# A decoder layer with PEER retrieval: another layout and place for the expert gates, more row gathers before the last stage, and scores computed a tile ahead

## The chip, the cores and the metric

The kernel runs on one core of a Trainium2 chip. The metric is the device time of one execution in microseconds (us); the kernel before takes 1810.99 us, the median of three runs (1809.59 to 1811.35).

## The reference

The layer handles 512 tokens of width 1024. Its first half (differential attention, an mLSTM branch, gates, an output projection) is not touched. The second half is PEER, a retrieval of single-neuron experts from a table of 128 x 128:

```
q = (ht @ w_q).reshape(T, 8, 2, 64)
s = einsum('thpd,pnd->thpn', q, sub_keys)
sv, si = top_k(s, 16)                      # per half key
cand = sv[:, :, 0, :, None] + sv[:, :, 1, None, :]
cv, ci = top_k(cand, 16)
eidx = i1 * 128 + i2                       # 16 experts of each of 8 heads
g = softmax(cv)
act = gelu(einsum('cd,chkd->chk', hc, u_tab[eidx]))
out = einsum('chk,chkd->cd', g * act, v_tab[eidx])
```

A residual, a scale by the condition's gate row (`gt2`) and a last LayerNorm follow.

## The kernel before, in words

The tokens are four tiles of 128. For tiles 1 to 3 (384 tokens) the kernel works densely: for each of the 128 expert blocks it multiplies all tokens by the block's 128 u rows, applies gelu, multiplies by a gate matrix that is zero where an expert was not chosen, and multiplies the result by the block's 128 v rows. Tile 0 is handled sparsely: for each of its 128 slots (8 heads x 16 experts) POOL gathers one u row per token with an indirect DMA of 512 KB (`fetch`, L861), and DVE takes the dot product with the hidden row (`dots`, L869); later 128 gathers of v rows are added up into `accg` (`sparse`, L1227). A generator is advanced by `some` (L882), with a credit, wherever the program has room for it.

Products are exact to about float32 by splitting each operand into two float16 parts and three matmuls (`mm3_one`). So each weight block that comes in as float32 (`raw`, `vraw`) is split by ACT (high part) and DVE (low part), `split` L167.

The stages that matter here:

* **Routing** (`route`, L940), one tile after the other. DVE picks the top 16 of every half key from the scores `sb` (L916 to L921), then the top 16 of 80 candidate sums, then builds one-hot matrices for 8 groups of 16 tokens (L1026 to L1037). PE turns each group into gates (`tr<-onehot`), ACT copies them into half of a staging tile (`gstage`, L1050) and writes them to DRAM as `gd` (L1054). The staging tile has two halves, so a group's first copy waits for the write of the group two before. PE's spare time is filled by u blocks 0 to 71, whose gelu results go to DRAM as `actd`. The scores of a tile's first bank are computed at the end of the tile before (tiles 2 and 3), those of the others one bank ahead (L941 to L947). In tiles 1 to 3 a dot of tile 0 is done after each bank and each group: 39 of the 128 in all. They use two gather buffers.
* **The stage change.** When routing is through, `h2d` (the hidden row's scale, saved earlier) is loaded, the row `gt2` is made by PE transposes (`gate_row`, L1188), six gate loads are issued, and then the first u block round.
* **The expert stage.** 32 rounds of 4 blocks; the order is rounds 18 to 31 and then 0 to 17. The first 14 compute their u products (`u_round`, L1270); the last 18 are "held", that is, their activations are loaded from `actd` (`act_load`). `v_round` (L1308) multiplies by v. `gate` (L1279) multiplies a round's activations `at` by the gates `gblk` on DVE and splits them. A gate block serves two rounds and comes in four loads of 384 KB (`gate_load`, L1254); `ahead` (L1262) issues loads two rounds early. Gathers per block: `SP_V` = 1 in a v block and `SP_U` - `SP_V` = 1.8 in a u block. In the last round (`last_part`) the rest of `sparse` is drained, with tile 0's final LayerNorm (`finish`).

All plain loads are issued by SP in one queue, in the order that the scheduler sets; ACT issues the writes to DRAM and POOL the gathers. Each engine works through its instructions in a fixed order, so an instruction that waits holds back all behind it.

Of the kernel before, what the change touches and what calls it, by code (L numbers as in the profile page):

```python
# [10 lines left out]
F32 = mybir.dt.float32  # L11
# [48 lines left out]
DOT_R = 1  # L60
SP_U = 2.8
SP_0 = 0
# [44 lines left out]
def body(tc, x, c, w_ada, b_ada, wz, wif, b_if, conv_w, conv_b, lam, subg, mlg,  # L107
# [6 lines left out]
    with pool(name="cst", bufs=1) as cst, pool(name="wts", bufs=1) as wts, \  # L114
# [222 lines left out]

        h2d = dr.tile([128, 1024], F32, name="h2d")
        with pool(name="fr", bufs=1) as fr:
# [499 lines left out]
        actd = dr.tile([N1 // 2, 128, 2 * TD], F32, name="actd")  # L839
        gd = dr.tile([TD // 16, 16, 128, 128], F32, name="gd")  # L840
        RU = 1.0 / (S_ACT * S_U)
# [19 lines left out]
        def fetch(table, e, k):  # L861
            b = ring["buf"]
            g_ = b[:, ring["n"] % b.shape[1]]
            ring["n"] += 1
            P.before(G.indirect_dma_start(out=g_, out_offset=None, in_=table,  # L865
                                          in_offset=bass.IndirectOffsetOnAxis(ap=e[:, k:k + 1], axis=0)))
            return g_
# [21 lines left out]
        with pool(name="rt", bufs=1) as rt:  # L889
            ring["buf"] = rt.tile([128, GB_R, 1024], F32, name="gat")  # L890
            ring["h2r"] = rt.tile([128, 1024], F32, name="h2rr")
# [48 lines left out]
            def route(t):  # L940
                sv = rtile("sv", [128, 16, 16])  # L941
                si = rtile("si", [128, 16, 16], U32)
                for n, (hq, p) in enumerate(banks):
                    if (t, hq, p) not in SB:
                        scores(t, hq, p)
                    if n < 3:
                        scores(t, *banks[n + 1])  # L947
                    sb = SB[t, hq, p]
                    for k in range(4):
                        w_ = rtile("tw", [128, 128])  # L950
                        e = 8 * hq + 2 * k + p
                        top16(sv[:, e], si[:, e], sb[:, k], w_)
                        yield FILL_S / 4
                    if t > 0:
                        some(dotg, DOT_S)
# [12 lines left out]
                for h in range(8):  # L968
                    cw_ = rtile("cw_", [128, 80])
                    top16(cv[:, h], ci[:, h], cd[:, h], cw_)  # L970
                    yield FILL_S / 4
                gk = rtile("gk", [128, 8, 16])
                V.tensor_sub(gk, cv, cv[:, :, 0:1].to_broadcast([128, 8, 16]))
# [19 lines left out]
                for m in range(2):  # L993
# [10 lines left out]
                    yield FILL_S  # L1004
                if 0 < t and t + 1 < NT:
                    scores(t + 1, 0, 0)
                if t == 0:
# [14 lines left out]
                for g in range(9):  # L1022
                    nxt = None
                    if g < 8:
                        s = slice(16 * g, 16 * g + 16)
                        oh = big([128, 3, 2048], F16, "onehot")  # L1026
                        o1 = oh[:, 0].rearrange("p (i t) -> p i t", t=16)
# [12 lines left out]
                    if pend is not None:  # L1040
# [3 lines left out]
                        for q4 in range(4):  # L1044
                            ps = ps_tr()
                            for k in range(4):
# [6 lines left out]
                            F.run(FILL_G)  # L1053
                        nc.scalar.dma_start(gd[8 * (t - 1) + pg].rearrange("b p f -> p b f"),  # L1054
                                            half.rearrange("p (b f) -> p b f", b=16))
# [105 lines left out]
            V.tensor_add(h2r, h2r, shr)  # L1161
            nc.scalar.dma_start(h2d, h2r)
            F.add("h2", weave(h2_part(1, 3), out3, H2_1))
# [12 lines left out]
            F.need("q_all")  # L1176
            stg = [big([128, 4096], F32, "gstage")]
            for t in range(1, NT):
                for ns in route(t):
                    F.run(ns)  # L1180
# [4 lines left out]
        rows = big([128, 4, 1024], F32, "rows2")  # L1185
        g2r, lg, lb, h2r = [rows[:, k] for k in range(4)]
        nc.sync.dma_start(h2r, h2d)
        gate_row(gt2, g2r)  # L1188
        with pool(name="vp", bufs=1) as vp:
# [4 lines left out]
            order = list(range(N1 // 4, 32)) + list(range(N1 // 4))  # L1194
            AT, WT, GB = {}, {}, {}

# [27 lines left out]

            ring["buf"], ring["h2r"] = gat, h2r

# [27 lines left out]
            def gate_load(n, k):  # L1254
                blk = order[n] // 2
                if blk not in GB:
                    GB[blk] = big([128, NG, 8, 16], F32, "gblk")
                gs = slice(k * NG // 4, (k + 1) * NG // 4)
                nc.sync.dma_start(GB[blk][:, gs].rearrange("p g e t -> p g (e t)"),
                                  gd[gs, blk].rearrange("g p f -> p g f"))  # L1260

# [8 lines left out]
            def u_round(n, rate=SP_U - SP_V):  # L1270
                at = new_at(n)
                for i in range(4):
                    for _ in u_gen(4 * order[n] + i, at[:, i]):
                        pass
                    if n == 0:
                        G.tensor_copy(gat[0:1, i, 0:1], at[0:1, i, 0:1])
                    some(sp, rate)

            def gate(n):  # L1279
# [4 lines left out]
                                op=ALU.mult)  # L1284
                w = vp.tile([128, 2, 4, TD], F16, name="w", tag="w", bufs=2)
                split(w[:, 0], w[:, 1], at, S_WT)
                WT[n] = w

# [44 lines left out]
            ops = []  # L1333
            for k in range(6):
                gate_load(k // 4 * 2, k % 4)
            u_round(0, SP_0)
            gate(0)
            for n in range(len(order)):
# [70 lines left out]
```

## Time and profile before

| | |
|---|---|
| median of three runs | 1810.99 us |
| the profiled execution | 1810.87 us, of which the span of the trace is 1808.8 us |
| first half of the layer | to about 560 us |
| routing | about 620 to 1030 us |
| stage change | about 1010 to 1060 us |
| expert stage with u blocks | 1060 to about 1450 us |
| held rounds | to about 1795 us |

In the rows further on, PE is TensorE, DVE is VectorE, ACT is ScalarE, POOL is GpSimd. SPq, ACTq and POOLq are the queues on which those engines issue DMAs. A time in square brackets at a row's end is how long the engine stood idle just before, and what released it.

### The profile page before, as it was taken

The page shows a single profiled execution, that of the slowest core. Times are in us where ns is not written, and L with a number is a line of the kernel's source. Part 1 is how long each engine was busy: PE and PEld are TensorE (multiplying, and loading weights), DVE is VectorE, ACT ScalarE, POOL GpSimd, SP SyncE. Part 2 cuts the span into 40 slices and gives each one's busy share as a digit, 9 for nine tenths or more (in the row PEclk, how much of TensorE's full clock was granted, in tenths as well). Part 3 has the DMA queues.
Part 4 walks back from the last instruction along what each step waited for, and adds up shares of the span by engine and source line. Part 5 has one row for each costly group of instructions (what it writes and reads, how often), then busy time and mean ns, then how long its engine had stood idle before and what let it go on. Part 6 is the DMA issues. An engine that isn't in the chain of part 4 may idle for free.

```text
span 1808.8 us, 26501 instructions
## 1 busy us (share of the span) xinstructions
PE 1704.3 (94%) x9937; PEld 915.9 (51%) x9937; DVE 1423.5 (79%) x2702; ACT 813.1 (45%) x1279; POOL 452.6 (25%) x296
## 2 busy tenths in 40 slices
PE   5999999989999989999998899999999998988996
PEld 2444455445444666766655555555555543433443
DVE  7787877697666798969989658888878777577796
ACT  4556666564343433636737543333333333232332
POOL 0000000000000100110210135554556445345551
PEclk9999999989999999999999999999999999999999
DMA  8554754347776536895976999999999999988982
GB/s 337 170 191 168 248 195 142 105 157 273 273 277 231 210 114 222 285 306 193 305 258 222 334 347 357 389 349 343 341 376 331 333 336 321 342 287 320 331 325 80
DMA packets 223104, 484.89 MB, mean 268 GB/s; under 512 B 16000, under 2 KB 114560, under 8 KB 222976
## 3 DMA queue, kind: packets, MB, share of 16 engines
q1 hardware_dynamic: 124912, 286.06, 46.0%
q0 software_dynamic: 36864, 134.23, 20.2%
q10 hardware_dynamic: 61200, 62.92, 10.1%
q8 instruction: 77, 1.26, 0.3%
q14 instruction: 51, 0.42, 0.1%
HBM read 418.14 MB, written 65.01 MB: 267 GB/s over the span
## 4 chain that ended last, share of the span: by engine, by line
PE 58%; DVE 16%; DMA 9%; issue 8%; POOL 4%; ACT 3%; ACTq 1%; SPq 0%; DVEq 0%; POOLq 0%
PE mm L101 32%; PE s L101 15%; PE tr L101 6%; POOL gat L865 3%; PE o L101 3%; DVE w L169 2%; DMA gat<-in_v_dram,ev 2%; DMA gd<-gstage 1%; PE tr L104 1%; DMA vraw<-in_v_dram 1%; DMA raw<-in_u_dram 1%; DVE accg L1235 1%; DVE gat L873 1%; ACTq L914 1%; DMA at<-actd 1%
## 5 line engine op out<-in xcount | busy, mean ns | idle before, releaser
L101 PEld LDWEIGHTS <-w 128*128 128x128 f16 x7176 | 690.5, 99 | 669.3 <-issue 30.1
L101 PE MATMUL mm<-h2T,w 128*128 128x384 f16 (+2 forms) x3288 | 558.0, 327 | 12.0 <-ACT ast L857 7.4
L101 PE MATMUL s<-w,w 128*128 128x512 f16 x1152 | 275.4, 384 | 25.7 <-DVE w L169 25.7
L865 POOL DMA_INDIRECT gat<-in_v_dram,ev x128 | 240.3, 1878 | 227.6 <-DVE accg L1235 210.9
L865 POOL DMA_INDIRECT gat<-in_urows_dram,eu x128 | 179.5, 1403 | 447.6 <-DVE gat L873 352.0
L169 DVE SCALAR_TENSOR_TENSOR w<-raw,w 128x1024 f16<-128x1024 f32 x180 | 218.8, 1219 | 73.6 <-ACT w L168 73.1
L168 ACT ACTIVATE w<-vraw 128x1024 f16<-128x1024 f32 x128 | 134.9, 1055 | 284.2 <-DMA vraw<-in_v_dram 158.4
L168 ACT ACTIVATE w<-raw 128x1024 f16<-128x1024 f32 x180 | 188.2, 1053 | 85.6 <-DMA raw<-in_u_dram 34.1
L101 PE MATMUL mm<-h1T,w 128*128 128x512 f16 x960 | 219.0, 379 | 1.8 <-DVE cva L624 1.8
L101 PE MATMUL tr<-w,w 128*128 128x512 f16 x768 | 187.0, 380 | 0.0
L169 DVE SCALAR_TENSOR_TENSOR w<-vraw,w 128x1024 f16<-128x1024 f32 x128 | 155.2, 1217 | 20.2 <-ACT w L168 20.0
L1235 DVE SCALAR_TENSOR_TENSOR accg<-gat,wg,accg 128x1024 f32<-128x1024 f32 x127 | 162.3, 1278 | 10.1 <-DMA gat<-in_v_dram,ev 9.5
L1283 DVE TENSOR_TENSOR at<-at,gblk 128x1536 f32<-128x1536 f32 x32 | 56.2, 1755 | 81.1 <-DMA at<-actd 70.7
L873 DVE SCALAR_TENSOR_TENSOR gat<-gat,rows 128x1024 f32<-128x1024 f32 x89 | 107.9, 1220 | 12.5 <-DMA gat<-in_urows_dram,eu 12.4
L101 PE MATMUL mm<-w,h1T 128*128 128x512 f16 x456 | 107.7, 382 | 3.6 <-ACT h1T L168 1.8
L101 PE MATMUL o<-w,w 128*128 128x512 f16 x384 | 105.4, 385 | 0.0
L101 PEld LDWEIGHTS <-h1T 128*128 128x128 f16 x672 | 58.3, 98 | 66.0 <-issue 2.5
L165 POOL TENSOR_TENSOR ss<-ss,mhalf 128x4 f32<-128x4 f32 x8 | 8.1, 1017 | 314.7 <-DVE ss L510 284.2
L857 ACT ACTIVATE at<-mm 128x384 f32<-128x384 f32 x56 | 27.4, 489 | 129.8 <-PE mm L101 126.3
L1050 ACT ACTIVATE gstage<-tr 128x512 f32<-128x512 f32 x96 | 56.5, 598 | 55.3 <-PE tr L101 37.9
L169 DVE SCALAR_TENSOR_TENSOR pre<-pre 128x1024 f16<-128x1024 f32 x44 | 53.8, 1222 | 31.4 <-ACT pre L168 30.6
L101 PEld LDWEIGHTS <-onehot 128*128 128x128 f16 x768 | 64.0, 148 | 19.6 <-issue 9.5
(460 smaller groups left out, 1837.0 us busy)
## 6 DMA issues: line engine op xcount, KB each, us to landing
vraw<-in_v_dram SPq DMA_DIRECT2D x128, 512.0 KB, 7.5
raw<-in_u_dram SPq DMA_DIRECT2D x92, 512.0 KB, 6.5
raw<-in_wz_dram SPq DMA_DIRECT2D x64, 512.0 KB, 4.3
w<-us SPq DMA_DIRECT2D x52, 512.0 KB, 4.5
wad<-in_w_ada_dram SPq DMA_DIRECT2D x48, 512.0 KB, 5.1
gd<-gstage ACTq DMA_DIRECT2D x24, 1024.0 KB, 9.3
gblk<-gd SPq DMA_DIRECT2D x64, 384.0 KB, 9.9
us<-pre ACTq DMA_DIRECT2D x44, 512.0 KB, 4.1
```

Of the source, the lines that this page charges most:

```text
L101: self._link(self.tc.nc.tensor.matmul(*a, **k))
L104: self._link(self.tc.nc.tensor.transpose(*a, **k))
L165: G.tensor_tensor(o, i, mhalf[:, :i.shape[1]], op=ALU.pow)
L168: A.activation(hi, src, AF.Copy, scale=scale)
L169: V.scalar_tensor_tensor(lo, src, scale, hi, op0=ALU.mult, op1=ALU.subtract)
L857: A.activation(dst, ps[:, :TD], AF.Gelu, scale=RU)
L865: P.before(G.indirect_dma_start(out=g_, out_offset=None, in_=table, in_offset=bass.IndirectOffsetOnAxis(ap=e[:, k:k + 1], axis=0)))
L873: V.scalar_tensor_tensor(g_, g_, 1.0, ring["h2r"], op0=ALU.mult, op1=ALU.mult, accum_out=wg[:, k:k + 1])
L914: nc.scalar.dma_start(actd[k], a.rearrange("p a b -> p (a b)"))
L1050: A.activation(st[:, :, 4 * q4:4 * q4 + 4], ps.rearrange("p t i -> p i t"), AF.Copy, scale=1.0 / S_G)
L1235: V.scalar_tensor_tensor(accg, g_, wg[:, k:k + 1], accg, op0=ALU.mult, op1=ALU.add)
L1283: V.tensor_tensor(av, av, GB[q_ // 2][:, :, e].rearrange("p g e t -> p e g t"), op=ALU.mult)
```

## The change

The gate array in DRAM is turned around: `gd` was [24 slots of 16 tokens, 16, 128, 128] and is now [16, 128, 24, 128]. A gate load then reads 3 KB runs instead of 512 B runs; the writes stay in 512 B pieces, and those of one partition now lie 1.5 MB apart (64 KB before), those of neighbouring partitions 12 KB apart (512 B before).

At the stage change the first four gate loads move into the last part of the first u round, behind its weights; `gt2`'s row is made early, beside the hidden row, and both come back in one load.

In routing, two more gather buffers lie in the fourth quarter of two fixed one-hot tiles; a dot is added after every second head's candidate selection in tiles 1 to 3 (12 more); and all four banks of the next tile's scores are computed at the end of a tile. In the expert stage `SP_U` is 3.0 instead of 2.8, so a u block carries 2 gathers instead of 1.8. One split tile (`WT[0]`) is allocated earlier.

```diff
-SP_U = 2.8
+SP_U = 3.0
-        h2d = dr.tile([128, 1024], F32, name="h2d")
+        h2d = dr.tile([128, 2, 1024], F32, name="h2d")
-        gd = dr.tile([TD // 16, 16, 128, 128], F32, name="gd")
+        gd = dr.tile([16, 128, TD // 16, 128], F32, name="gd")
...
         def fetch(table, e, k):
-            b = ring["buf"]
-            g_ = b[:, ring["n"] % b.shape[1]]
+            g_ = ring["buf"][ring["n"] % len(ring["buf"])]
...
-                    if n < 3:
+                    if n < 3 and (t, *banks[n + 1]) not in SB:
                         scores(t, *banks[n + 1])
...
                     top16(cv[:, h], ci[:, h], cd[:, h], cw_)
                     yield FILL_S / 4
+                    if t > 0 and h % 2 == 1:
+                        some(dotg, DOT_S)
...
-                if 0 < t and t + 1 < NT:
-                    scores(t + 1, 0, 0)
+                if t == 0:
+                    F.need("q_all")
+                if t + 1 < NT:
+                    for hq in range(2):
+                        for p in range(2):
+                            scores(t + 1, hq, p)
...
-                        oh = big([128, 3, 2048], F16, "onehot")
+                        oh = OH[g % 2]
...
-                        nc.scalar.dma_start(gd[8 * (t - 1) + pg].rearrange("b p f -> p b f"),
+                        nc.scalar.dma_start(gd[:, :, 8 * (t - 1) + pg].rearrange("b p f -> p b f"),
...
-            nc.scalar.dma_start(h2d, h2r)
+            nc.scalar.dma_start(h2d[:, 0], h2r)
+            g2s = t4("g2s")
+            gate_row(gt2, g2s)
+            nc.scalar.dma_start(h2d[:, 1], g2s)
...
+            OH = [big([128, 4, 2048], F16, "onehot") for _ in range(2)]
+            ring["buf"] = ([gat_[:, k] for k in range(GB_R)]
+                           + [oh[:, 3].bitcast(F32) for oh in OH])
...
-        g2r, lg, lb, h2r = [rows[:, k] for k in range(4)]
-        nc.sync.dma_start(h2r, h2d)
-        gate_row(gt2, g2r)
+        h2r, g2r, lg, lb = [rows[:, k] for k in range(4)]
...
-                nc.sync.dma_start(GB[blk][:, gs].rearrange("p g e t -> p g (e t)"),
-                                  gd[gs, blk].rearrange("g p f -> p g f"))
+                nc.sync.dma_start(GB[blk][:, gs].rearrange("p g e t -> p (g e t)"),
+                                  gd[blk][:, gs].rearrange("p g f -> p (g f)"))
...
+                    if n == 0 and i == 3:
+                        for k in range(4):
+                            gate_load(0, k)
+                        nc.sync.dma_start(rows[:, 0:2], h2d)
...
-            for k in range(6):
-                gate_load(k // 4 * 2, k % 4)
             u_round(0, SP_0)
+            for k in range(2):
+                gate_load(2, k)
             gate(0)
```

How the scheduler's order moves is shown at three places. The first is SP's queue at the stage change. `raw` are u weights, `vraw` v weights, `gblk<-gd` gate loads, `rows<-h2d` the saved rows. Before:

```order
L1187 DMA rows_10955<-h2d 128x1024
L173 DMA raw<-in_u_dram 128x1024 x2
L1259 DMA gblk<-gd 128x6x128 x3
L173 DMA raw<-in_u_dram 128x1024 x2
L1259 DMA gblk<-gd 128x6x128 x3
L173 DMA raw<-in_u_dram 128x1024 x2
L1259 DMA gblk<-gd 128x6x128
L1295 DMA vraw<-in_v_dram 128x1024 x2
```

In the changed kernel, the same stretch of the same queue:

```order
L173 DMA raw<-in_u_dram 128x1024 x43
L1309 DMA vraw<-in_v_dram 128x1024
L1269 DMA gblk<-gd 128x768 x4
L1290 DMA rows_10973<-h2d 128x2048
L1269 DMA gblk<-gd 128x768 x3
L1309 DMA vraw<-in_v_dram 128x1024
```

Four u weight loads that stood among the gate loads now stand ahead of all of them, and the saved rows have moved behind the first four gate loads.

The second place is ACT's order where tile 1's one-hot groups end and tile 2's selection begins. `sb<-s` brings a bank of scores from PSUM, `ast<-mm` the gelu of a u block. Before:

```order
L1050 ACTIVATE gstage<-tr 128x128x4 x4
L857 ACTIVATE ast<-mm 128x384
L1054 DMA gd<-gstage 128x16x128
L914 DMA actd<-ast 128x768
L934 ACTIVATE sb<-s 128x512
L857 ACTIVATE ast<-mm 128x384
L934 ACTIVATE sb<-s 128x512
```

In the changed kernel the four banks stand in one piece ahead of tile 1's first one-hot group:

```order
L857 ACTIVATE ast<-mm 128x384
L933 ACTIVATE sb<-s 128x512 x4
L857 ACTIVATE ast<-mm 128x384
L168 ACTIVATE w_8963<-raw 128x1024
L913 DMA actd<-ast 128x768
L168 ACTIVATE rT<-tr 128x128
L1037 ACTIVATE onehot<-rT 128x2048 x2
```

They no longer stand behind the two DMA issues at the end of the tile.

The third place is DVE's order where tile 0's sum ends. `accg<-gat,wg,accg` adds one gathered v row, `at<-at,gblk` is a round's gate product. Before, four sums and the LayerNorm of tile 0 stand among the last results `fo`:

```order
L169 SCALAR_TENSOR_TENSOR w_16293<-vraw,w_16293 128x1024
L1235 SCALAR_TENSOR_TENSOR accg<-gat,wg,accg 128x1024 x4
L1330 SCALAR_TENSOR_TENSOR fo<-s,rows_10955 128x512
L1235 SCALAR_TENSOR_TENSOR accg<-gat,wg,accg 128x1024
L1202 TENSOR_TENSOR fo<-fo,ax_5393 128x512
L1238 TENSOR_TENSOR accg<-accg,rows_10955 128x512 x2
```

In the changed kernel they end with five rounds of v blocks still to come:

```order
L1245 SCALAR_TENSOR_TENSOR accg<-gat,wg,accg 128x1024
L1297 TENSOR_TENSOR at<-at,gblk 128x1536
L1248 TENSOR_TENSOR accg<-accg,rows_10973 128x512 x2
L1212 TENSOR_TENSOR accg<-accg,ax_5393 128x512 x2
L169 SCALAR_TENSOR_TENSOR w_15902<-vraw,w_15902 128x1024
```

## Rows read from the trace of the kernel before

**Rows 1.** The page, part 1: busy time, share of the span, instructions

```profile
PE 1704.3 (94%) x9937; PEld 915.9 (51%) x9937; DVE 1423.5 (79%) x2702; ACT 813.1 (45%) x1279; POOL 452.6 (25%) x296
```

**Rows 2.** Stretches: length, busy PE, PEld, DVE, ACT, POOL; granted clock; DMA share; GB/s

```profile
680.00:800.00 120.00, 118.59 (x922) 79.47 (x921) 96.84 (x325) 53.55 (x76) 14.40 (x13) 1.00 0.85 275
800.00:920.00 120.00, 115.68 (x890) 76.58 (x889) 110.34 (x298) 72.84 (x97) 16.62 (x13) 1.00 0.80 261
920.00:1000.00 80.00, 73.37 (x515) 47.05 (x514) 79.76 (x224) 44.32 (x58) 8.78 (x7) 0.96 0.68 216
1000.00:1060.00 60.00, 50.58 (x370) 33.95 (x368) 31.65 (x34) 30.19 (x43) 6.44 (x7) 0.91 1.02 333
1060.00:1440.00 380.00, 380.00 (x2056) 201.05 (x2055) 319.40 (x355) 142.73 (x168) 208.60 (x140) 1.00 0.97 353
...
1480.00:1720.00 240.00, 214.26 (x952) 94.39 (x951) 173.51 (x137) 76.70 (x69) 119.75 (x55) 0.96 0.90 321
```

**Rows 3.** Timeline of the stage change: start, duration, engine, instruction, idle before

```profile
1024.86 4.69 SPq L1259 DMA_DIRECT2D gblk<-gd  x3
...
1039.30 1.06 ACT L168 ACTIVATE w<-raw 128x1024 f16<-128x1024 f32 x1 [5.42 <-DMA raw<-in_u_dram]
...
1040.90 1.12 PE L104 MATMUL tr<-ident,mcgt 128*128 128x128 f32 x4 [4.28 <-ACT gstage L1050]
...
1041.80 17.84 PE L101 MATMUL mm<-h2T,w 128*128 128x384 f16 x96
```

**Rows 4.** Waits, 1480 to 1720 us: us in total, times, longest

```profile
DVE at L1283 <- DMA at<-actd: 63.7, 8, 11.3
...
PE s L101 <- DVE w L169: 25.7, 7, 5.4
```

**Rows 5.** Timeline of a held round, SP's queue and DVE

```profile
1567.74 3.35 SPq L1251 DMA_DIRECT2D at<-actd  x2
...
1582.31 1.76 DVE L1283 TENSOR_TENSOR at<-at,gblk 128x1536 f32<-128x1536 f32 x1 [10.46 <-DMA at<-actd]
```

**Rows 6.** Tile view of actd: the load issued at 1567.74, then the pair at 1554.5

```profile
DMA to landing us min/median/max: 13.5/13.5/13.5
...
DMA to landing us min/median/max: 3.6/3.9/4.2
```

**Rows 7.** DMA issues, 1480 to 1720 us: count, KB each, median us to landing

```profile
at<-actd SPq DMA_DIRECT2D x28, 384.0 KB, 5.4
gblk<-gd SPq DMA_DIRECT2D x24, 384.0 KB, 9.8
```

**Rows 8.** The page, part 3: queue, packets, MB, share of 16 engines' span

```profile
q0 software_dynamic: 36864, 134.23, 20.2%
q10 hardware_dynamic: 61200, 62.92, 10.1%
```

**Rows 9.** Instruction groups by shape: count, busy us, mean ns, idle before

```profile
L873 DVE SCALAR_TENSOR_TENSOR gat<-gat,h2rr 128x1024 f32<-128x1024 f32 x39 | 47.3, 1214 | 4.8 <-DMA gat<-in_urows_dram,eu 4.8
...
L873 DVE SCALAR_TENSOR_TENSOR gat<-gat,rows 128x1024 f32<-128x1024 f32 x89 | 107.9, 1220 | 12.5 <-DMA gat<-in_urows_dram,eu 12.4
```

**Rows 10.** Timelines where tiles 2 and 3 begin, and PE in tile 3

```profile
794.25 0.49 DVE L917 MAX8 sv<-sb 128x8 f32<-128x128 f32 x2 [7.81 <-ACT sb L934]
...
916.01 0.49 DVE L917 MAX8 sv<-sb 128x8 f32<-128x128 f32 x2 [5.21 <-ACT sb L934]
...
954.88 7.41 PE L101 MATMUL mm<-h2T,w 128*128 128x384 f16 x28 [5.17 <-ACT ast L857]
```

**Rows 11.** Timeline of the end

```profile
1784.41 1.28 DVE L1238 TENSOR_TENSOR accg<-accg,rows 128x512 f32<-128x512 f32 x2
...
1789.58 5.34 PE L101 MATMUL tr<-w,w 128*128 128x512 f16 x24
...
1804.40 1.41 DVE L1221 SCALAR_TENSOR_TENSOR fo<-fo,rs,rows 128x512 f32<-128x512 f32 x2
```

**Rows 12.** Tile view of gstage: the gate writes' time to landing

```profile
DMA to landing us min/median/max: 5.8/9.3/14.3
```

More of the change, by code (lines that the diff above doesn't have):

```diff
@@ L889, in body @@
         with pool(name="rt", bufs=1) as rt:
-            ring["buf"] = rt.tile([128, GB_R, 1024], F32, name="gat")
+            gat_ = rt.tile([128, GB_R, 1024], F32, name="gat")
             ring["h2r"] = rt.tile([128, 1024], F32, name="h2rr")
@@ L1194, in body @@
             order = list(range(N1 // 4, 32)) + list(range(N1 // 4))
-            AT, WT, GB = {}, {}, {}
+            AT, GB = {}, {}
+            WT = {0: vp.tile([128, 2, 4, TD], F16, name="w", tag="w", bufs=2)}
             def finish(t, o, halves):
@@ L1223, in finish @@
                     nc.sync.dma_start(out[0, t * 128:(t + 1) * 128, s], o[:, s])
-            ring["buf"], ring["h2r"] = gat, h2r
+            ring["buf"], ring["h2r"] = [gat[:, k] for k in range(4)], h2r
             def sparse():
@@ L1284, in gate @@
                                 op=ALU.mult)
-                w = vp.tile([128, 2, 4, TD], F16, name="w", tag="w", bufs=2)
-                split(w[:, 0], w[:, 1], at, S_WT)
-                WT[n] = w
+                if n not in WT:
+                    WT[n] = vp.tile([128, 2, 4, TD], F16, name="w", tag="w", bufs=2)
+                split(WT[n][:, 0], WT[n][:, 1], at, S_WT)
             ACC = [[ps_s(), ps_s()], [ps_s(), ps_o()],
```

## The prediction

> **What bounds the kernel now.** I read the page first: PE is busy 94% of the span [rows 1], so a change gains only where PE idles or runs below full clock, or in the tail. The table of stretches then says where that is [rows 2]. Between 1060 and 1440 us PE is busy for the whole 380 us: the rounds with u blocks are bound by PE, though the DMA engines stand at a share of 0.97 beside it. The other stretches lose time. Idle PE time is 120 - 118.59 = 1.4 us, then 4.3 and 6.6 us in routing (680 to 1000), 9.4 us at the stage change (1000 to 1060) and 25.7 us in the held rounds (1480 to 1720). Where PE has idled, the granted clock falls from full (2.4 GHz): its mean of 0.96, 0.91 and 0.96 costs a further 0.04 x 80 = 3.2, 0.09 x 60 = 5.4 and 0.04 x 240 = 9.6 us. So the places that the change touches lose 15.5 us in routing, 14.8 us at the stage change and 35.3 us in the held rounds.
>
> The waits of the held rounds name the cause [rows 4]: PE waits seven times, 25.7 us, for a split weight from DVE, and DVE waits eight times, 63.7 us, in front of the gate product `at<-at,gblk` for the load of `at`. The timeline shows one such wait [rows 5]: the loads of `at` are issued at 1567.74, and DVE stands until 1582.31. That load took 13.5 us to land; the pair before it, with no gate loads ahead of it in SP's queue, took about 3.9 us [rows 6]. The gate product stands on DVE ahead of v splits, so PE starves, once in two rounds, because four gate loads are queued ahead of `at`.
>
> **The change, part by part.** The sum is made against the profiled execution, 1810.87 us; the median is 0.12 us longer. About 0.2% (3.6 us) is what a measurement can tell from no change.
>
> *Packet prices.* The gather queue's 36864 packets are 256 gathers x 128 runs of 4 KB, and completions of no weight; 20.2% x 16 x 1808.8 us = 5846 engine-us [rows 8], so 178 ns per 4 KB run. ACT's queue has 2923 engine-us. Taking off 45 writes x 128 runs of 4 KB (1025) and 36 x 128 of 3 KB at three quarters of that (617) leaves 1281 for 24 x 2048 = 49152 pieces of 512 B: 26 ns each. A gate load is now 768 x 26 = 20.0 engine-us and becomes 128 x 134 = 17.2, 0.18 us over 16 engines; four loads, which stand ahead of one `at`, save 0.7 us.
>
> *Gather count.* Of the 256 gathers, 39 dots are done in routing [rows 9] and 217 are left. After the change 51 are done and 205 left. Thirteen rounds with u blocks take 4 x 2.8 = 11.2 each now (145.6), and 12 then (156). So 71.4 are left for the held rounds now, 49 then; at four a round that is 17.9 rounds against 12.3. In the last five v rounds before the final one no gather competes with the loads and no sum stands on DVE.
>
> *Held rounds: -13 us.* Each of seven PE waits costs 35.3 / 7 = 5.0 us. Of these, about 1.5 fall in rounds that are now free of gathers. The other 5.5 get shorter by what the gate loads ahead of `at` save. The lower bound is nothing; the upper is the difference between a gate load's landing and that of an `at` load of the same 384 KB, 9.8 - 5.4 = 4.4 us [rows 7]. I take 1 us, near the packet price, because the two medians also differ by place in the queue. That leaves 5.5 x 4.0 = 22 of 35 us. The bounds give -7.5 and -32.
>
> *Rounds with u blocks: +1 us.* Added are 10.4 gathers x 128 x 178 ns / 16 = 14.8 us of all DMA engines; 26 gate loads give back 4.7. Over some 400 us the share goes from 0.97 to nearly 1.00. DVE has room (319 of 380 us [rows 2]; the added sums and dots cost 10.4 x 1.3 = 13.5). I take almost nothing, since PE has not idled at 0.97; the bound is the whole of the 10 us.
>
> *Stage change: -8 us.* SP spends 4.7 us at 1024.86 on issues of gate loads that wait for gate writes; the u weights behind them are late, ACT waits 5.42 us for one, and its gate copies, then PE's transposes for the `gt2` row, wait behind that: 4.28 us [rows 3]. In the new order those weights precede the gate loads, and the transposes (1.1 us of PE and more for a first half) are gone. I count 4.3, the transposes at 1.7 and half of the 5.4 us of clock, rounded down to 8. Late next is the first gate product, which stands on DVE ahead of v splits and whose last gate load can only go when the last gate write has landed, about 9.3 us after its issue [rows 12]; the first u round of 15 to 18 us [rows 3] covers the write and part of the load. If the load is 4 to 6 us late, the gain is 3. Upper bound 14.8.
>
> *Routing: -4 us.* Twelve dots add 12 x (1214 ns + some 80 for the accumulator) = 15.6 us to DVE [rows 9]. In tiles 2 and 3 DVE idles 7.81 and 5.21 us for the first scores [rows 10], because their copies stand on ACT behind two DMA issues; with all four banks a tile early that goes, 13 us. DVE is full between 920 and 1000 (79.76 of 80), but PE, which bounds the stage, idles only where ACT is held up, for example 5.17 us at 954.88. DVE starting earlier against PE's backlog should save some of the 15.5 us. Bounds: -15.5, and +10 if tile 3's dots and those of tile 2 (5.2 us each) go straight through. Two more gather buffers remove nothing on PE's path: DVE waited for a routing gather only 4.8 us in all [rows 9].
>
> *Tail: -4 us.* PE ends at 1794.92, and the last DVE instruction starts at 1804.40 [rows 11]. In between DVE still has the other tiles' results, since tile 0's finish (eight half-width operations of about 0.65 to 0.7 us, and a last sum of 1.28: 6.6 us) stood ahead of them. That moves five rounds forward, beside PE. Bounds 0 and -6.6.
>
> *Early `gt2` row: +1 us.* Two more ACT copies of 0.6 us and a write, ahead of tile 0's routing, where DVE is the engine that is waited for.
>
> Sum: -13 + 1 - 8 - 4 - 4 + 1 = -27, so 1784 us.
>
> **Rule against row.** The rows say that a 512 B piece costs 26 ns where an eighth of a 4 KB run costs 22, so merging pieces gains a little. The Trainium skill ("DMA: Bandwidth & Descriptors", Specifications) gives 512 B as the size from which a transfer already runs at line rate. By that rule the 3 KB runs bring nothing, the held term falls to -7.5 and the sum to about 1789; the trace half agrees, as 26 is near 22.
>
> **The rivals.**
>
> 1. *All three waits vanish*, 17%. If gate loads land like `at` loads, DVE's wait no longer reaches PE: held -32. With the clock then full in routing (-10) and at the change (-13), the tail at -4 and the early row at +1, the sum is -58: 1753 us. For it: the 4.4 us of [rows 7]. Against it: a DMA share of 0.97 and 0.90 with little room.
> 2. *The DMA engines bind*, 14%. The u rounds pay 10 us, the held rounds gain only 7.5, routing 0, the change 6, the tail 3, early row 1: -5.5, so about 1805 us. For it: the share near 1.00. Against it: PE did not idle once at 0.97.
> 3. *The gate writes become slow, and it is slower*, 9%. Their pieces lie 12 KB and 1.5 MB apart now. A staging half is reused two groups later, and writes land after 9.3 us, up to 14.3 [rows 12]; every us more is paid by the first copy of 18 groups (eight per tile, less the first two). If the spread costs them the 4.4 us that lies between scattered and whole reads [rows 7], that is 18 x 4.4 = 79 us: 1863 us. From 27 / 18 = 1.5 us on, that is a landing of 10.8 us, it eats the whole gain. For it: no row shows such a write. Against it: the pieces are as many and as large as before.
>
> The page named above (Latency and other measured facts) reports slow rows only for a partition pitch of 512 KiB and more at powers of two; 12 KB is none, so by it this rival falls away. No run here shows it.
>
> **How the numbers follow.** My forecast case (1765 to 1800) has 60%. Predicted: 1784 us. The range takes in the second rival and most of the way to the first: 1758 to 1808; outside lie the third rival, half of the first and a little of the second. Faster by over 0.2%: 0.60 + 0.17 + 8 of the second's 14 = 0.85; within 0.2%: 0.04; slower: 0.09 and 0.02 of the second, 0.11.
>
> **What would show it.** In the trace after: DVE's wait for `at` with five or six entries, each about 1 us shorter, and none in the last five rounds; no wait of the first selection of a tile for `sb`; no PE gap of 4 us before the first u round; 380 of 380 us PE in the u rounds; the median landing of a gate load nearer to 5 than to 10 us, and of a gate write still near 9. I am wrong if PE idles in the u rounds, if gate writes land later, or if routing ends later by more than the dots' 15.6 us.

## The result and the profile after

The changed kernel takes 1820.78 us (median of four runs, 1819.14 to 1821.51) against 1810.51 us before: a ratio of 1.0059, 95% interval 1.0044 to 1.0074. It is slower by 0.6%; I had forecast 1.5% faster. The profiled execution has a span of 1817.2 us, 8.4 more than before. The page's first part, which answers to [rows 1], shows the same work:

```profile
PE 1707.7 (94%) x9937; PEld 917.4 (50%) x9937; DVE 1421.2 (78%) x2702; ACT 811.8 (45%) x1279; POOL 451.8 (25%) x296
```

The stretches of [rows 2] in the changed kernel, in the same columns:

```profile
680.00:800.00 120.00, 115.24 (x884) 77.06 (x882) 113.16 (x412) 55.43 (x78) 23.62 (x18) 0.99 0.86 278
800.00:920.00 120.00, 105.72 (x776) 68.77 (x774) 98.77 (x286) 61.87 (x81) 16.36 (x13) 0.94 0.76 247
920.00:1000.00 80.00, 72.61 (x466) 44.58 (x465) 69.25 (x168) 40.90 (x53) 16.16 (x12) 0.96 0.77 266
1000.00:1060.00 60.00, 58.92 (x511) 42.56 (x509) 48.79 (x51) 41.67 (x58) 5.24 (x4) 1.00 0.92 288
1060.00:1440.00 380.00, 375.70 (x2025) 198.99 (x2025) 313.08 (x338) 136.62 (x165) 222.23 (x143) 0.99 0.98 370
...
1480.00:1720.00 240.00, 219.52 (x973) 96.66 (x974) 181.88 (x146) 76.81 (x69) 110.04 (x54) 0.95 0.89 338
```

PE's idle time between 680 and 1000 has grown from 12.4 to 26.4 us, and its clock has fallen from 1.00 to 0.94 in the second stretch. Between 1000 and 1060 PE is busy, but with routing that is late. The held rounds have gained 5.3 us of busy PE.

A window of fixed times mixes stages when one of them moves. So this table gives marks on PE's timeline instead: the start of the last group of eight one-hot matmuls, the first u round's start (192 matmuls back from the next mark), the first v matmul, and PE's end, each in us from the start of that kernel's profiled execution. The last columns are the time from the first v matmul to PE's end, and the span. All kernels but the first two are experiments that are told below. Each row is a single execution, up to 7.4 us from its kernel's median (dots_only 1837.31 against 1829.87 us, gd_only 1800.80 against 1794.06); in the first mark, three kernels with the same routing code but for the gate writes' addresses (before, gd_only, spu_only) lie 3.5 us apart. So a difference of two or three us between two rows says little.

| kernel | last one-hot | first u round | first v matmul | PE's end | v to end | span |
|---|---|---|---|---|---|---|
| before | 1034.7 | 1041.8 | 1075.5 | 1794.9 | 719.4 | 1808.8 |
| changed | 1049.8 | 1050.8 | 1090.5 | 1805.4 | 714.9 | 1817.2 |
| old_routing | 1035.5 | 1036.4 | 1074.7 | 1786.2 | 711.5 | 1798.0 |
| routing_only | 1049.2 | 1055.2 | 1090.4 | 1808.5 | 718.2 | 1819.9 |
| dots_only | 1061.8 | 1069.9 | 1104.2 | 1823.8 | 719.6 | 1835.2 |
| scores_only | 1032.7 | 1041.5 | 1074.9 | 1794.0 | 719.1 | 1807.8 |
| gd_only | 1037.0 | 1039.8 | 1076.7 | 1784.8 | 708.1 | 1798.7 |
| v_old_gd | 1036.9 | 1037.9 | 1075.8 | 1807.5 | 731.7 | 1819.3 |
| spu_only | 1033.5 | 1042.8 | 1077.0 | 1802.5 | 725.5 | 1813.9 |
| v_spu28 | 1034.0 | 1035.0 | 1074.2 | 1776.1 | 701.9 | 1790.4 |
| stage_only | 1034.3 | 1035.3 | 1072.8 | 1793.1 | 720.3 | 1807.4 |
| v_late_g2 | 1031.3 | 1032.3 | 1070.5 | 1782.3 | 711.8 | 1793.6 |
| v_actd_sp | 1034.8 | 1035.8 | 1072.2 | 1787.9 | 715.7 | 1799.7 |
| best | 1029.2 | 1030.2 | 1065.9 | 1771.0 | 705.1 | 1784.9 |
| gate_act | 1029.9 | 1030.9 | 1067.2 | 1761.7 | 694.5 | 1776.2 |

Take the first two rows. Routing ends 15.1 us later. From there to the first u round 6.1 us are saved (7.1 before, 1.0 now), and the first two u rounds take 6.0 us more (39.7 against 33.7). The expert stage is 4.5 us shorter, the tail 2.1 (11.8 against 13.9). Together that is +8.4. So the loss is in routing, and the expert stage gives back a third of the 13 us I had put on its held rounds.

Who waits in routing (waits from 680 to 1060 us: total, times, longest):

```profile
DVE cd L959 <- DMA actd<-ast: 14.6, 1, 14.6
...
PE tr L101 <- DVE onehot L1038: 7.2, 6, 3.1
...
PE tr L101 <- DVE onehot L1042: 5.9, 5, 2.0
```

PE now waits eleven times for one-hot products of DVE, 13.1 us (1.4 us in the same window before). And once DVE itself stands still for 14.6 us, because `cd` takes the slot of an `ast` tile (both rotate through the same four) whose write was issued late. That issue stands in ACT's timeline, with the next gelu behind it (the experiments below tell whether this stall costs anything):

```profile
797.73 10.38 ACTq L913 DMA_DIRECT2D actd<-ast  x1
...
808.22 0.87 ACT L857 ACTIVATE ast<-mm 128x384 f32<-128x384 f32 x2 [10.59 <-issue]
```

The stage change in the timelines of ACT and PE; the last line is the mark "first v matmul":

```profile
1055.62 3.24 ACTq L913 DMA_DIRECT2D actd<-ast  x1
1063.76 0.87 ACT L857 ACTIVATE at<-mm 128x384 f32<-128x384 f32 x2 [3.79 <-DMA actd<-ast]
1064.30 26.32 PE L101 MATMUL mm<-h2T,w 128*128 128x384 f16 x144 [4.67 <-ACT at L857]
1090.46 2.11 PE L101 MATMUL s<-w,w 128*128 128x512 f16 x9
```

The gap of 4.28 us ahead of the first u round [rows 3] is gone, and a gap of 4.67 us inside that round has come: the first `at` tiles wait until the last write of `actd` has landed, and that one is issued behind the last gate write.

The waits of the held rounds, 1480 to 1720 us, which answer to [rows 4]:

```profile
DVE at L1297 <- DMA at<-actd: 56.3, 8, 9.7
PE s L101 <- DVE w L169: 16.0, 7, 4.8
PE s L101 <- ACT w L168: 4.7, 1, 4.7
```

### The profile page after: what moved, and what is told of

Read it like the earlier page. It is cut to its first block, busy times and chain, and to the rows that moved or that the text cites. A ratio compares the mean times of both kernels' runs of the same rounds, so it can differ in the third digit from the quotient of the medians.

```text
span 1817.2 us, 26498 instructions
## 1 busy us (share of the span) xinstructions
PE 1707.7 (94%) x9937; PEld 917.4 (50%) x9937; DVE 1421.2 (78%) x2702; ACT 811.8 (45%) x1279; POOL 451.8 (25%) x296
## 4 chain that ended last, share of the span: by engine, by line
PE 36%; DVE 24%; DMA 17%; issue 11%; POOL 8%; ACT 3%; ACTq 1%; SPq 0%; DVEq 0%; POOLq 0%
PE mm L101 21%; PE s L101 10%; POOL gat L864 7%; DMA gat<-in_v_dram,ev 6%; DVE w L169 5%; DVE accg L1245 4%; DMA at<-actd 3%; PE tr L101 3%; DMA vraw<-in_v_dram 2%; PE o L101 2%; DMA actd<-ast 1%; ACTq L913 1%; PE tr L104 1%; DMA raw<-in_u_dram 1%; DMA pre<-in_u_dram 1%
## 5 line engine op out<-in xcount | busy, mean ns | idle before, releaser
L864 POOL DMA_INDIRECT gat<-in_v_dram,ev x128 | 233.0, 1821 | 185.6 <-DVE accg L1245 172.3
L864 POOL DMA_INDIRECT gat<-in_urows_dram,eu x103 | 157.0, 1524 | 261.6 <-DVE gat L872 162.7
L872 DVE SCALAR_TENSOR_TENSOR gat<-gat,rows 128x1024 f32<-128x1024 f32 x77 | 93.8, 1222 | 31.9 <-DMA gat<-in_urows_dram,eu 31.8
L101 PE MATMUL tr<-onehot 128*128 128x128 f16 x768 | 66.1, 229 | 16.2 <-DVE onehot L1038 7.2
```

The source lines that it names most:

```text
L101: self._link(self.tc.nc.tensor.matmul(*a, **k))
L872: V.scalar_tensor_tensor(g_, g_, 1.0, ring["h2r"], op0=ALU.mult, op1=ALU.mult, accum_out=wg[:, k:k + 1])
```

## The experiments

Ratios are to the kernel before on the same chip, with 95% intervals; 0.1% is 1.8 us. Single differences under 0.3% are inside the intervals, and where one matters the marks stand beside it. The theory to begin with was that routing lost the time, through dots or early scores in DVE's chain; the rival, that the turned-around gate array did, through slower gate writes. "Routing edits" are the 12 dots, the two added gather buffers with the fixed one-hot tiles, and the early scores.

### Routing

**old_routing** takes all routing edits back in the changed kernel; **routing_only** makes them alone in the kernel before.

```diff
-                    if t > 0 and h % 2 == 1:
-                        some(dotg, DOT_S)
...
-                        oh = OH[g % 2]
+                        oh = big([128, 3, 2048], F16, "onehot")
...
-                if t == 0:
-                    F.need("q_all")
-                if t + 1 < NT:
-                    for hq in range(2):
-                        for p in range(2):
-                            scores(t + 1, hq, p)
+                if 0 < t and t + 1 < NT:
+                    scores(t + 1, 0, 0)
```

> The changed kernel with the three routing edits taken back (12 dots fewer, two gather buffers and a new one-hot tile per group, scores one bank ahead). Theory 1, routing is what lost: the last gate write goes back from 1055 to about 1044 us and the time falls by 12 to 18 us, to 1803 to 1809. Rival, the turned-around gate array loses it (slower gate writes hold ACT): the time stays within 4 us of 1821.

> The kernel before with the three routing edits alone. Theory 1: slower than before by 10 to 16 us (1821 to 1827), with the one-hot matmuls of PE waiting for DVE. Rival (gate array): within 3 us of 1811.

Measured: 0.9957 (0.9932 to 0.9981) and 1.0056 (1.0034 to 1.0078). Taking them back gains about 1% (18 us), and alone they cost 0.6% (10 us). That routing loses the time is shown from both sides; the rest of the change is a gain.

**no_dots** takes back only the first hunk, **old_scores** only the last (with the condition at the bank), **old_bufs** only the buffers and one-hot tiles, all in the changed kernel. **dots_only** and **scores_only** make the first and the last alone in the kernel before; **scores_late** is scores_only without its first case, tile 1's scores and the early query weights:

```diff
-                if t == 0:
-                    F.need("q_all")
-                if t + 1 < NT:
+                if 0 < t and t + 1 < NT:
```

> The changed kernel without the 12 dots after candidate selection; the gathers left are drained later. Theory 1a, the dots' 15.6 us of DVE are what routing lost: 1806 to 1813. Rival 1b, the loss is in the two fixed one-hot tiles, the buffers or the early scores: 1817 to 1823.

> The changed kernel with the scores one bank ahead, as before, and the query weights not asked for early. Theory 1a (dots): within 4 us of 1821, either way. Rival 1c, the four banks ahead take PE's and ACT's place from the u blocks: 1809 to 1815, and the start up to 680 us gives back its 3 us.

> The changed kernel with two gather buffers and a new one-hot tile per group, as before. Theory, the buffers carry nothing: 1.004 to 1.008 of the kernel before, as the changed kernel itself. Rival, the two fixed one-hot tiles hold PE and POOL up: 1.000 to 1.003.

> The kernel before with the 12 dots after candidate selection and nothing else. Theory 7, DVE bounds tiles 2 and 3, so that most of their 15.6 us reaches the end of routing: 5 to 10 us slower, 1.003 to 1.006. Rival, they cost only beside the early scores: within 3 us, 0.999 to 1.001.

> The kernel before with the four banks of scores a tile ahead and the query weights asked for early, and nothing else. Theory 6, the scheduler can now place the next tile's selection on DVE among this tile's one-hot products, so PE waits for one-hots: 7 to 12 us slower, 1.004 to 1.007 of the kernel before, with PE waits for one-hot operations of 8 us and more in routing. My forecast (DVE's waits for scores go, PE gains): 4 to 10 us faster, 0.994 to 0.998.

> The same, but only at the end of tiles 1 and 2: tile 1's scores and the query weights stay where they were. Theory 6: nearly the same loss, 5 to 10 us, 1.003 to 1.006, since tile 1's one-hot stage with tile 2's selection in it is unchanged. Rival, the early query weights delay the start and are what costs: 0.999 to 1.001.

| kernel | ratio | interval |
|---|---|---|
| no_dots | 1.0011 | 0.9993 to 1.0029 |
| old_scores | 1.0002 | 0.9988 to 1.0015 |
| old_bufs | 1.0066 | 1.0044 to 1.0088 |
| dots_only | 1.0093 | 1.0058 to 1.0128 |
| scores_only | 1.0008 | 0.9994 to 1.0021 |
| scores_late | 1.0031 | 1.0011 to 1.0051 |

Alone, the dots cost most: 17 us (by the interval 10 to 23), about the 15.6 us of DVE that they take. The last one-hot group comes 27 us later in that profile, which is of the longest of its four runs. Its waits (620 to 1075 us) and the stretch of [rows 2] that suffers most:

```profile
PE tr L104 <- DVE ii L1005: 14.0, 5, 4.7
...
DVE gat L873 <- DMA gat<-in_urows_dram,eu: 12.1, 6, 3.8
...
PE mm L101 <- ACT ast L857: 11.4, 5, 5.5
```

```profile
920.00:1000.00 80.00, 63.80 (x392) 37.32 (x391) 68.36 (x239) 35.92 (x46) 10.42 (x10) 0.91 0.74 252
```

PE waits 14.0 us for `ii` (0.9 us before), the expert numbers at the end of DVE's chain of selection, which the dots stand in; and where a dot waits for its gather (12.1 us against 5.5 in the same window before), the chain waits with it. PE is down to 63.80 of 80 us at a clock of 0.91 (73.37 at 0.96 before [rows 2]).

The early scores do what I expected of them and gain nothing by it. DVE's wait for scores falls from 18.2 to 4.2 us (same window, before and scores_only), but a new wait has come:

```profile
PE tr L101 <- DVE onehot L1037: 8.5, 5, 4.7
...
DVE sv L917 <- ACT sb L934: 4.2, 2, 2.7
```

The reason stands in DVE's order. Before, tile 2's selection follows tile 1's one-hot products as a block. With the scores there early, the scheduler sets most of its steps between the products, each ahead of a one-hot that PE needs. Theory 6 had 7 to 12 us for this and measured 1.4; its mechanism is seen, its size is not. In scores_late the loss is 5.6 us with an interval down to 2, so what it leaves out, the early query weights among it, is not what costs. old_bufs is no faster than the changed kernel, so nothing hangs on the buffers and tiles there. It also settles the stall of DVE shown above: in old_bufs that wait is 2.5 us and the time is no better, and in no_dots it is 14.2 us and the time is 9 us better, so the stall is not what routing loses.

The parts do not add up in every order. Taking the scores back in the changed kernel gains about 10 us, where alone they cost 1; taking the dots back gains 9, where alone they cost 17, and that is more than the 10 us of all three edits together (the intervals overlap). So in the changed kernel neither part is the main one, against my expectation for old_scores, and how the 18 us divide stays open. Each kernel is a new order of some 26000 instructions, and no run here separates that from the edits.

### The layout of the gate array

**v_old_gd** undoes it in old_routing; **gd_only** makes it alone in the kernel before.

```diff
-        gd = dr.tile([TD // 16, 16, 128, 128], F32, name="gd")
+        gd = dr.tile([16, 128, TD // 16, 128], F32, name="gd")
```

> The changed kernel with the routing edits and the turned-around gate array taken back, so gate loads in 512 B runs. My price, 0.7 us for each at load that stands behind four gate loads and 1 us taken: the held rounds lose 3 to 6 us, 0.997 to 0.999 of the kernel before. Rival, the layout does nothing (line rate from 512 B): 0.9957. Rival, gate loads of whole runs land like at loads: slower by 10 us and more, 1.002.

> The kernel before with the gate array turned around and nothing else. Theory 4, gate loads of 3 KB runs let the at loads behind them land earlier: the expert stage from the first v matmul to PE's end goes from 719 to about 702 us, 0.990 to 0.993 of the kernel before. My forecast's price (0.7 to 1 us for each at load): 0.997. Rival, the pieces' size does nothing: 1.000.

Measured: 1.0043 (1.0025 to 1.0060) against old_routing's 0.9957, and 0.9911 (0.9880 to 0.9943) alone. Both say about 16 us, three times the 5.5 that I gave it. The time from the first v matmul to PE's end is 20.2 us shorter in the first pair and 11.3 in the second. The gate loads in the held rounds (count, KB, median us to landing) in v_old_gd, then in v_late_g2, which has the new layout:

```profile
gblk<-gd SPq DMA_DIRECT2D x25, 384.0 KB, 10.0
```

```profile
gblk<-gd SPq DMA_DIRECT2D x24, 384.0 KB, 9.0
```

A median 1 us shorter for each of four loads ahead of an `at` is worth more than 1 us to it. PE's stalls there come once in two rounds, and go from 36.2 us apart in v_old_gd to 34.2 in old_routing (means of five distances in PE's timeline). That is 2 us for each of some eight; PE's own work of two rounds is 31.0 us, eight v blocks that start 3.88 us apart where nothing waits. So the price by packets was right in sign and too small. It came from mean packet times of other queues; the packets of these loads themselves, between 1480 and 1720 us, took 28.6 ns for 512 B in v_old_gd and 128.4 ns for 3 KB in old_routing (means over the trace's DMA records). So 768 of the one against 128 of the other are 1.4 us over 16 engines for four loads, not 0.7.

And the price left out what the small pieces do to SP. Its timeline around four gate loads in v_old_gd, and then in old_routing:

```profile
1613.70 4.10 SPq L1301 DMA_DIRECT2D vraw<-in_v_dram  x1
1617.84 0.43 SPq L1261 DMA_DIRECT2D gblk<-gd  x1
1618.37 3.11 SPq L1253 DMA_DIRECT2D at<-actd  x2
```

```profile
1598.22 0.33 SPq L1301 DMA_DIRECT2D vraw<-in_v_dram  x1
1598.60 0.43 SPq L1261 DMA_DIRECT2D gblk<-gd  x1
1601.09 0.80 SPq L1253 DMA_DIRECT2D at<-actd  x2
```

Behind gate loads of 512 B runs, the issue of a v weight takes 4.10 us instead of 0.33 and that of two `at` loads 3.11 instead of 0.80. Between 1480 and 1720 us, 17 issues of SP take over 1 us each in v_old_gd and 13 in the kernel before, 45.1 and 35.6 us in all; in old_routing and gd_only it is one each, of 1.35 and 1.03 us. So the second `at` load is out 11.3 us after the first of four gate loads in v_old_gd, and 7.1 us in old_routing. How the 16 us divide between these issues and the loads' own time, no run separates. One of them stands in [rows 5], 3.35 us for two issues; the prediction has no term for it.

The gate writes, which the third rival feared, are not slower: ACT's wait for them to free `gstage` is 7.3 us in v_old_gd and 7.4 in old_routing, and 15.6 before and 11.9 in gd_only.

By the Trainium skill ("DMA: Bandwidth & Descriptors", Specifications) pieces of 512 B already run at line rate, and 3 KB runs would have brought nothing. The runs say 16 us for the same bytes; the measurement decides.

### Two gathers in a u block

**v_spu28** undoes it in old_routing, **spu_only** makes it alone.

```diff
-SP_U = 2.8
+SP_U = 3.0
```

> The changed kernel with the routing edits taken back and 1.8 gathers in a u block as before, so that gathers run on into the last held rounds. My price: rounds freed of gathers save 7.5 us and tile 0's finish 4 us, so this is 8 to 12 us slower, 1.000 to 1.003 of the kernel before. Rival, gathers do not matter in the held rounds: 0.9957 with the tail's 2 to 4 us lost, 0.997.

> The kernel before with two gathers in a u block instead of 1.8 and nothing else. Theory 5, the denser u rounds use up the lead of the v weights, and PE starves from the first held round on: slower by 9 to 13 us, 1.005 to 1.007 of the kernel before, with PE waits between 1440 and 1480 where there are none now. My forecast's price for the rounds freed of gathers and the tail: faster by 8 to 11 us, 0.994 to 0.996.

Measured: v_spu28 0.9920 (0.9890 to 0.9949), so 7 us faster than with 3.0 (the intervals overlap, but the time from the first v matmul to PE's end says 9.6), and spu_only 1.0035 (1.0011 to 1.0058), 6 us slower. The stretch 1440 to 1480 before, and then in spu_only:

```profile
1440.00:1480.00 40.00, 40.00 (x201) 19.46 (x199) 26.88 (x22) 13.06 (x14) 17.09 (x9) 1.00 0.97 350
```

```profile
1440.00:1480.00 40.00, 34.41 (x166) 16.45 (x165) 30.77 (x25) 11.82 (x13) 21.41 (x13) 0.91 0.94 338
```

The timelines of DVE and PE there:

```profile
1455.21 1.76 DVE L1283 TENSOR_TENSOR at<-at,gblk 128x1536 f32<-128x1536 f32 x1 [8.01 <-DMA at<-actd]
...
1468.94 0.60 PE L101 MATMUL s<-w,w 128*128 128x512 f16 x2 [2.51 <-ACT w L168]
1472.62 3.17 PE L101 MATMUL s<-w,w 128*128 128x512 f16 x7 [3.08 <-DVE w L169]
```

At the handover DVE now waits 8.01 us for the first held round's `at` (4.55 in the kernel before, at 1446.09), the v splits behind it are late, and PE idles 5.6 us and runs at 0.91. The u rounds themselves show no more than 0.82 us of idle PE, at the second one's start: the added gathers used up the lead that these rounds build, and it is missing where the next rounds need it. What was to pay for it did not exist. In the changed kernel the last gathered row is added at 1715.4 us, 90 us before PE's end; in the kernel before PE's last wait of the held rounds ends 95 us before its end, and behind it PE does not wait, with the gathers beside it:

```profile
1700.25 2.40 PE L101 MATMUL s<-w,w 128*128 128x512 f16 x7 [3.68 <-DVE w L169]
```

So rounds freed of gathers had nothing to gain. (In spu_only and old_routing, which lack the 12 dots, the last row is added only 45 and 48 us before PE's end.)

### The stage change

**stage_only** makes it alone, with the early row. **v_late_g2** puts the row behind the first u round in old_routing, **v_actd_sp** moves one write in old_routing:

```diff
-                nc.scalar.dma_start(actd[k], a.rearrange("p a b -> p (a b)"))
+                (nc.sync if k == N1 // 2 - 1 else nc.scalar).dma_start(
+                    actd[k], a.rearrange("p a b -> p (a b)"))
```

> The kernel before with the stage-change edits alone (gate loads behind the first u round, early gt2 row, both rows in one load). Theory 3: the gap ahead of the first u round goes (4 to 5 us), but the first at tiles wait for the last actd write and the start of routing loses 2.6 us: within 3 us of the kernel before, 0.998 to 1.002. My forecast: 7 us faster, 0.996.

> The changed kernel with the routing edits taken back, and the gt2 row made at the end of the first u round instead of early. Theory 2, the early row costs the start of routing about 2.6 us of PE idle (51.6 of 60 us busy between 620 and 680, against 54.1 before): 2 to 4 us faster than with the routing edits alone taken back, 0.993 to 0.995 of the kernel before. Rival, the start is only reordered and the transposes on PE in the first u round give it back: no difference, 0.9957.

> The changed kernel with the routing edits taken back, and the last write of actd issued by SP instead of ACT, where it stands behind the last gate write. Theory 3, the stage change is now held by that write's landing, since the first at tiles wait for it: PE's gap of 4.7 us in the first u round goes, 3 to 6 us faster than without this edit, about 0.993 of the kernel before. Rival, the gate product or the u weights are late next: the gap stays over 3 us.

Measured: 1.0005 (0.9983 to 1.0027), 0.9925 (0.9897 to 0.9952) and 0.9921 (0.9892 to 0.9949). The stage change by itself is neutral: in stage_only the first u round starts 6.5 us earlier and the expert stage ends 1.8 us earlier. Without the early row routing ends 4.2 us sooner (1031.3 against 1035.5), so the row costs more than the 1 us I gave it; the interval of the ratio overlaps old_routing's, but the first mark bears it out in more profiles: 1034.0 to 1036.9 in the five kernels with the early row and routing as before, 1029.2 to 1031.3 in the three with the late one. In v_actd_sp, PE:

```profile
1044.86 4.06 PE L101 MATMUL mm<-h2T,w 128*128 128x384 f16 x24 [1.10 <-ACT at L857]
1050.99 21.34 PE L101 MATMUL mm<-h2T,w 128*128 128x384 f16 x120 [2.08 <-ACT at L857]
```

The gap of 4.66 us in old_routing has become 1.10 and 2.08, a third less and in sum still over the rival's 3 us. The write's place in ACT's queue was at most that third; ACT's wait for its landing remains (4.09 us, 4.1 in old_routing), so theory 3 holds only in part. The intervals of the ratios overlap.

### The gains put together

**best** is the layout and the stage change, with SP_U 2.8, the late row, the `actd` write on SP and routing as before. **gate_act** adds one line:

```diff
-                nc.sync.dma_start(GB[blk][:, gs].rearrange("p g e t -> p (g e t)"),
+                (nc.scalar if held(n) else nc.sync).dma_start(
+                                  GB[blk][:, gs].rearrange("p g e t -> p (g e t)"),
```

> The gate array turned around and the gate loads behind the first u round, with the last write of actd on SP, the gt2 row made in the first u round, 1.8 gathers in a u block and routing as before. If the gains of the single edits add up: 0.986 to 0.989 of the kernel before, about 1786 to 1791 us. Rival, the held rounds are again the next bound and eat what the stage change gives: 0.991 to 0.993.

> The best kernel so far with the gate loads of the held rounds issued by ACT instead of SP, so that no at load stands behind a gate load in its queue. Theory 8, what DVE waits for in the held rounds is the place in SP's queue: DVE's wait for at (56 us between 1440 and 1790 in that kernel) falls below 20 us, PE's 14 us of waits with it, 8 to 14 us faster than that kernel, 0.981 to 0.985 of the kernel before. Rival, the DMA engines' total is what binds there: 0.988 to 0.991, the wait moves to another load. Rival, a gate load that waits for its slot holds up ACT's splits: over 0.992.

Measured: 0.9893 (0.9865 to 0.9921), 1789 us, and 0.9861 (0.9842 to 0.9880), 1783 us. Both beat both kernels; between the two the intervals overlap, and the time from the first v matmul to PE's end is 10.6 us shorter in gate_act's profile. The held rounds (stretch, and waits 1480 to 1720) in best and then in gate_act:

```profile
1480.00:1720.00 240.00, 225.69 (x1019) 100.09 (x1018) 182.98 (x144) 79.05 (x71) 119.17 (x58) 0.98 0.90 334
...
DVE at L1288 <- DMA at<-actd: 54.5, 10, 9.5
PE s L101 <- DVE w L169: 14.3, 6, 3.8
```

```profile
1480.00:1720.00 240.00, 231.18 (x1068) 103.73 (x1067) 194.00 (x154) 87.00 (x79) 125.52 (x61) 1.00 0.93 351
...
DVE at L1289 <- DMA at<-actd: 40.3, 9, 8.2
PE s L101 <- DVE w L169: 8.8, 6, 2.4
```

With the gate loads out of SP's queue the bytes are the same, but the loads behind them wait less: DVE's wait for `at` falls by 14 us, not to under 20 as theory 8 had it, and PE's from 14.3 to 8.8 us, at full clock. The place in the queue is a part of what the held rounds wait for. That the engines' total, at a DMA share of 0.93, is the rest is likely but not shown. The Trainium skill ("DMA: Bandwidth & Descriptors", Rules for kernel authors) says that spreading DMAs over issuing engines only saves issue time. Here it also changed what the `at` loads stand behind, and 334 GB/s became 351.

## Why the prediction was wrong, point by point

* **What bounds the kernel**: right for the held rounds; v_old_gd, gd_only and gate_act all move the time through the late `at`. For routing it was wrong: I read "PE bounds the stage" from its busy share.
* **Held rounds, -13 us.** The sum hides two terms of opposite sign. The layout was -5.5 and measured about -16: its direction was right, but the 1 us for each `at` load was too small, since the packets alone gave 1.4 and SP's long issues behind small pieces stood in no term. The gate load's landing, which I expected nearer to 5 us than to 10, was 9.0 in v_late_g2. The rounds freed of gathers were -7.5, and 3.0 gathers measured +6: here the step "1.5 of seven waits fall in rounds that are now free" failed, as all seven waits lie ahead of those rounds.
* **u rounds, +1 us.** PE's row there was right (375.70 of 380; the rest is the gap at the stretch's start). That a lead is used up there and paid for later was missing.
* **Stage change, -8 us.** It measured 0, with the early row in it. I named the first gate product as late next; late next was the landing of the last `actd` write, whose memory the first `at` takes.
* **Routing, -4 us.** It measured about +18 in the changed kernel and +10 alone, at my bound of +10 or past it. The step that failed, and with it the forecast, is the set-off of the dots' 15.6 us against 13 us of DVE's waits for first scores. The dots stand in DVE's chain, at whose end PE waits, and cost 17 us alone; the waits for scores did go, but their place was taken by selection steps among the one-hots, so nothing was left to set the dots off against (scores_only +1.4, where -13 us of DVE had been counted).
* **Tail, -4 us**: -2.1 by the marks. **Early row, +1 us**: about 4.
* **The rivals.** The gate writes are not slow, the DMA engines do not stop PE in the u rounds, and the waits of the held rounds do not vanish. None of my rivals had routing itself as the loser, though my own bounds for it reached to +10. My sign of being wrong there, routing ending later by more than 15.6 us, did not quite come: it ended 15.1 us later.

## What to carry to other kernels

An engine that is busy 95% of a stage need not set its pace: before work is put on another engine as free, look whether a chain there ends in something that the busy one waits for, and if so, price the work at its full length. A stage that shows no wait may be building a lead that the next one needs, so the price of more load is looked for at the handover. And a change of several parts is tried part by part, for here about -16 and between +10 and +18 us stood in one diff. Last, a DMA of many small pieces is priced with what is issued behind it in the same queue, not by its packets alone.

## What the runs showed of the hardware

* For the same 384 KB and the same bytes in all, loads in 3 KB runs instead of 512 B made the kernel about 16 us faster. A 512 B packet of a load took 28.6 ns (v_old_gd), a 3 KB packet 128.4 ns (old_routing), which is 21.4 ns per 512 B.
* A DMA's issue can take long when DMAs of many small pieces stand just ahead of it in its queue, and the issuing engine stands still for that time. On SP's queue it was up to 4.42 us behind gate loads of 768 pieces in v_old_gd, and at most 1.35 us behind the same loads in 128 pieces (old_routing). On ACT's queue a write of `actd` took 10.38 us at 797.73, directly behind the gate write of 2048 pieces at 797.27, and 5.96 us at such a place in the kernel before; the usual issue takes 0.33 to 0.37 us.
* In the held rounds of the kernel before, PE's three waits of 4.70 to 5.38 us were each followed by slow matmuls, the three of 1.83 to 3.07 us were not. A row of gate_act's held rounds, and then one of the kernel before; the seven matmuls are the same:

```profile
1636.12 1.69 PE L101 MATMUL s<-w,w 128*128 128x512 f16 x7 [2.35 <-DVE w L169]
```

```profile
1519.01 3.17 PE L101 MATMUL s<-w,w 128*128 128x512 f16 x7 [5.09 <-DVE w L169]
```

The granted clock is 1.00 (2.4 GHz) in the first row and 0.50 (1.2 GHz) in the second, and over 1480 to 1720 us 1.00 in the one kernel and 0.96 in the other. The length of the wait does not decide alone: in best one of 2.18 us was followed by the same seven matmuls in 3.17 us. So shortening a stall can give back more than its own length.
